# A hybrid decoder block on one core: residual rows and half of each attention output added by transfers, and the last recurrence head's gate kept in another buffer

## The chip, the cores and the metric

The kernel runs on one core of a Trainium2 chip. The metric is the device time of one launch in microseconds (us), on the core. TensorE (PE) multiplies matrices into PSUM, VectorE (DVE) and ScalarE (ACT) compute and empty PSUM, GpSimd (POOL) computes on SBUF alone, SyncE (SP) issues transfers (DMAs) that 16 DMA engines carry out. All engines run their own instructions in order and wait for each other by semaphores.

## What is computed

One layer on x with 1024 rows of 1024 columns in float32. After a normalisation one input projection feeds two groups of heads; their outputs are concatenated, go through one output projection, and are added to x. Then follow a normalisation, a SwiGLU network of 2816 hidden columns, and a last normalisation. Cut to what matters here:

```python
u = rmsnorm(h, norm1_w[l])
proj = jnp.einsum('bsd,de->bse', u, w_in[l])
ya = dilated_attention_group(qa, ka, va)          # 8 heads of 64, three patterns merged
yb = hgrn2_group(qb, fb, ib, gb, lb_table[l], hgrn_norm_w[l])   # 4 heads of 128, gated linear recurrence
mixed = jnp.concatenate([ya, yb], axis=-1).astype(h.dtype)
h = h + jnp.einsum('bse,ed->bsd', mixed, w_out[l])
u2 = rmsnorm(h, norm2_w[l])
gu = jnp.einsum('bsd,df->bsf', u2, w_gate_up[l])
gate, up = gu[..., :FFN_HIDDEN], gu[..., FFN_HIDDEN:]
h = h + jnp.einsum('bsf,fd->bsd', jax.nn.silu(gate) * up, w_down[l])
return rmsnorm(h, final_norm_w)
```

In `hgrn2_group` each head's output is normalised and multiplied by `silu(g)`, the gate.

## The kernel before

Matrices are multiplied to float32 accuracy by splitting each operand into a high and a low part (`hi` copies to the rounded format, `lo` subtracts), and multiplying three of the four pairs. The large projections use one level of Strassen.

The program does not issue its instructions directly. `Prog` collects operations with an engine or a choice of engines, a cost, and the buffers that each reads and writes; `schedule` is a list scheduler that plays all operations through on a model of the engines and fixes the order of each engine's queue. An operation has a class (`P.cls`): the recurrence (`hgrn`) is class 0, attention is class 1, the rest is class 2, and within a class the longest remaining chain goes first. A transfer lands, in that model, behind all transfers issued before it, 2.2 us plus its own length after the end of its issue. `flex` lets the planner choose between engines: additions that read PSUM are DVE's alone, copies out of PSUM by `hi` or `act` are ACT's, the scaling of probabilities (`ts`) may go to DVE or POOL. So a change of costs or dependences can change the order of everything behind it.

The stages overlap. The input projection runs first and spills its results to DRAM tensors (`f_d`, `q_d`, `g_d` and so on). The four recurrence heads run beside it. Each `hgrn(h)` keeps the decays `f` and the keys or states `ks` in the buffer `E14`, and the intra-chunk scores `A` and the values `iv` in `E16`. When the scores have been used by the last products (`po`), it loads the gate `g_d` over `A` (line 945), forms the mean squares, POOL takes the power (`rstd_of`, line 379), ACT scales, PE transposes, DVE multiplies by the gate (line 311), and SP stores to `m_d`, the concatenated outputs.

Attention runs over 8 heads and, within each, four blocks `j` of 256 queries. DVE takes the masked maximum of the scores (line 1017), ACT the exponentials, POOL or DVE scale by the reciprocal sum (line 320), PE transposes the probabilities (line 1054), ACT and DVE split them (lines 353 and 307), and PE multiplies with the values. The values' high and low halves stand side by side as 128 columns, so the product `py` is a 128 x 256 PSUM tile whose lower 64 partitions hold the high part's product and whose upper 64 the low part's. The output is the sum of both halves. There are 32 such tiles. The slots `ya` and `yb` are two 256-column parts of a buffer with the tag `lm`. Head groups follow each other two at a time; the last are heads 6 and 7 with blocks 2 and 3.

The output projection (`out_proj`, class 2) fills gaps of PE in the attention. It runs per block of 128 tokens (`t`): first with the blocks of 128 rows 0, 1, 2 of `m_d` (recurrence heads 0 to 2), later with blocks 3 to 6, and last with block 7 (attention heads 6 and 7). Each pass accumulates in PSUM and adds to the residual `ht`, a half (512 columns) at a time, on DVE. The residual starts as x, loaded by four transfers of 1 MB into `E13`, `E6`, `E15` and `E16`. The FFN with its own normalisation follows.

Of the kernel before, what the change touches and what calls it, by code (L numbers as in the profile page):

```python
# [13 lines left out]
AF = mybir.ActivationFunctionType  # L14
OP = mybir.AluOpType
# [5 lines left out]
D = 1024  # L21
# [50 lines left out]
class Prog:  # L72
# [44 lines left out]
    class Clock:  # L117
# [7 lines left out]
        def to(self, t):  # L125
            while t >= (self.win + 1) * self.W:
                share = self.busy / self.W
                self.fast = share > 0.42 if self.fast else share > 0.84
                self.win, self.busy = self.win + 1, 0.0
# [123 lines left out]
def hymba_block(ctx: ExitStack, tc: tile.TileContext, x, norm1_w, w_in, lb_logits, hgrn_norm_w, w_out,  # L253
                norm2_w, w_gate_up, w_down, final_norm_w, cos, sin, amask, lmask, eye, out):
    nc = tc.nc
    x = x[0]
    out = out[0]
# [5 lines left out]
    P = Prog()  # L263
# [5 lines left out]
    def moved(nbytes, run):  # L269

        return nbytes / run * (0.008 + run / 27e3) / 16

    def dma(o, i, nbytes, run=2048):
        r = [i] if isinstance(i, (View, Buf)) else []
        w = [o] if isinstance(o, (View, Buf)) else []
        gi = i if r else (lambda: i)
        go = o if w else (lambda: o)
        P.op("SP", 0.5, lambda: nc.sync.dma_start(go(), gi()), r, w, nbytes=moved(nbytes, run))

    def mm(items, r, w):  # L280
        cost = sum(4 * n / 2400.0 + 0.008 if f32 else n / 2400.0 + (0.0132 if n > 128 else 0.007)
                   for o, lt, rh, st, sp, n, m, f32 in items)

        def fn():
            for o, lt, rh, st, sp, n, m, f32 in items:
                nc.tensor.matmul(o(), lt(), rh(), start=st, stop=sp, skip_group_check=True)  # L286
        P.op("PE", cost, fn, r, w)
# [9 lines left out]
    def bank_of(x):  # L297
        return (x.buf if isinstance(x, View) else x).pool == "ps"

    def two(n, psum=False):  # L300

        dve = ("DVE", 0.07 + n * 1.04e-3, not psum)
        return [dve] if psum else [dve, ("POOL", 0.17 + n * 2.1e-3, True)]

    def tt(eng, o, a, b, op, n, f=1.0):
        alts = two(n, bank_of(a) or bank_of(b) or bank_of(o) or op == OP.max)
        P.flex(alts, lambda e: ENG[e].tensor_tensor(o(), a(), b(), op=op), [a, b], [o])  # L307
# [16 lines left out]
    def act(o, a, func, n, scale=1.0, bias=None, accum=None):  # L324
        r, w, kw = [a], [o], {}
        cost = (0.06 if a.buf.pool == "ps" else 0.095) + n * 0.83e-3
        for k, s in (("scale", scale), ("bias", bias)):
            if isinstance(s, View):
                r.append(s)
                cost += 0.09  # L330
        if accum is not None:
            w.append(accum)
            cost += 0.09

        def fn():
            kw = {}
            if isinstance(scale, View) or scale != 1.0:
                kw["scale"] = scale() if isinstance(scale, View) else scale
            if bias is not None:
                kw["bias"] = bias()  # L340
            if accum is not None:
                kw["accum_out"] = accum()
            nc.scalar.activation(o(), a(), func, **kw)  # L343
        P.op("ACT", cost, fn, r, w, aset=SETS.get(func))
# [16 lines left out]
    whole = lambda b: b.v(lambda t: t)  # L361
# [9 lines left out]
    lm = P.buf("lm", [128, 10, 64], I32)  # L371
# [24 lines left out]
    def bank(stream, shape=(128, 512)):  # L396
        names = BANKS[stream]
        while True:
            n = rot[stream] = rot.get(stream, -1) + 1
            tag = f"b{names[n % len(names)]}"  # L400
            if tag not in held:
                return P.buf(tag, list(shape), F32, "ps")

    def turn(name, n):
        rot[name] = rot.get(name, -1) + 1
        return rot[name] % n
# [10 lines left out]
    def E(i, shape, dt=F32):  # L417
        return P.buf(f"E{i}", shape, dt)

    def colv(b, a, n, key):  # L420
        return b.v(lambda t: t[:, a:a + n], key)
# [10 lines left out]
    m_d = P.buf("m_d", [D, S], F32, "dr")  # L432
# [73 lines left out]
    def mm3(o, lh, ll, rh, rl, start, stop, n, m=128):  # L506
        return [(o, lh, rh, start, False, n, m, False), (o, lh, rl, False, False, n, m, False),
                (o, ll, rh, False, stop, n, m, False)]
# [321 lines left out]
    def hgrn(h):  # L830
        rs = slice(h * 128, h * 128 + 128)
        f, ks = colv(E14, 0, S, 0), colv(E14, S, S, 1)
        qp = colv(E15, 0, S, 0)
        A, iv = colv(E16, 0, S, 0), colv(E16, S, S, 1)
# [19 lines left out]
        def scores(n, g):  # L854

            ps = bank("h", (128, 2, 192))
            mm([(ps.v(lambda b, c=c: b[:, c, :n]), cs(ks, 2 * g + c),
                 E15.v(lambda t, c=c: t[:, S + (2 * g + c) * 192:S + (2 * g + c) * 192 + n]),
                 True, True, n, 128, True) for c in range(2)], [half(ks, g // 2), E15.v(None, 1)], [ps])
            return ps  # L860
# [31 lines left out]
        for g in range(4):  # L892
            ps = scores(192, g)
# [7 lines left out]
        for i, l in enumerate((1, 3, 5)):  # L901
# [8 lines left out]
            for g in range(4):  # L910
                ps = scores(192, g)
# [14 lines left out]
        for g in range(2):  # L926
            ps = bank("h")
# [9 lines left out]
        for c in range(NT):  # L937
            o = pj(po[c // 4], c % 4)
# [3 lines left out]
                it.append((o, cs(qp, c), cs(ks, c - 1), False, True, 128, 128, True))  # L942
                rd += [half(qp, c // 4), half(ks, (c - 1) // 4)]
            mm(it, rd, [o])
        gt = A
        dma(gt, g_d.v(lambda b: b[rs, :], h), 128 * S * 4)
        ss = P.buf("hss", [128, NT])
        for g in range(2):
# [14 lines left out]
    ys = []  # L963
# [23 lines left out]

    def attention(h, js):
        G = h // 4
        yb, ya = ys  # L990
        EQ, EV = EA[h % 2]
        qs, kh = colv(EQ, 0, S, 0), colv(EQ, S, S, 1)
        vv, kl = colv(EV, 0, S, 0), colv(EV, S, S, 1)
# [5 lines left out]
        for j in js:  # L999
            pr = {}  # L1000
            for b in (2 * j, 2 * j + 1):
                mx = None
                for g in range(b // 4 + 1):
                    n = min(512, (b + 1) * 128 - g * 512)
                    ps = bank("s")
# [6 lines left out]
                    p = probs()  # L1012
                    pn = p.buf.v(lambda t, p=p, n=n: p.get(t)[:, :n], p.key)
                    m = P.buf("mx%d" % turn("mx", 6), [128, 1])
                    o = 896 - b * 128 + g * 512
# [11 lines left out]
                for g in range(ng):  # L1027
                    p, pn, n = pr[b, g]
# [5 lines left out]
                for g in range(ng):  # L1034
                    p, pn, n = pr[b, g]
                    ts("POOL", pn, pn, whole(ri), 0.0, n)
            py = bank("y", (128, 256))
            for m2 in range(j + 1):
                diag = m2 == j
                n = 384 if diag else 512  # L1040
                pt = bank("t")
                many, col, rd = [], 0, set()
                for kb in (2 * m2, 2 * m2 + 1):
                    for b in (2 * j, 2 * j + 1):
                        if kb <= b:
                            p = pr[b, kb // 4][0]
# [22 lines left out]
                    it.append((py.v(lambda t, oc=oc: t[:, oc]), EV.v(lambda t, kb=kb: t[:, kb * 128:kb * 128 + 128], 0),  # L1069
                               tl.v(lambda t, cc=cc: t[:, cc]), False, last, nn, 128, False))  # L1070
                mm(it, [vh, vl, th, tl], [py])
            act(yb, py.v(lambda t: t[64:128, :]), AF.Copy, 256)
            act(ya, py.v(lambda t: t[:64, :]), AF.Copy, 256)
            tt("POOL", ya, ya, yb, OP.add, 256)
            dma(m_d.v(lambda b, j=j: b[512 + h * 64:576 + h * 64, j * 256:j * 256 + 256], (4 + h // 2, j // 2, h % 2, j % 2)), ya, 64 * 256 * 4, 1024)

    P.cls = 0
    for h in range(4):
        hgrn(h)
    P.cls = 1  # L1080
    yab = P.buf("lm", [64, 512])
    ys += [colv(yab, 256 * i, 256, i) for i in range(2)]
    dma(amv, amask, 128 * 1920 * 4)
    for h, js in [(h + i, js) for h in (0, 2, 4) for js in ((0, 1, 2), (3,)) for i in range(2)] + [
            (6, (0, 1)), (7, (0, 1)), (6, (2, 3)), (7, (2, 3))]:
        attention(h, js)
# [24 lines left out]
    def out_proj(t, *parts):  # L1111
        ht = hp[t]
        ks = [k for _, p, _ in parts for k in p]
        for n in range(2):
            ps = bank("o")
            for m, k, off in [(m, k, off) for m, p, off in parts for k in p]:
                lh, ll = (v.buf.v(lambda b, v=v, off=off: v.get(b)[:, off:off + 128]) for v in m[k])
                rh, rl = (v.buf.v(lambda b, v=v, n=n: v.get(b)[:, n * 512:n * 512 + 512], v.key) for v in WO[k])
                mm(mm3(whole(ps), lh, ll, rh, rl, k == ks[0], k == ks[-1], 512), [*m[k], *WO[k], *([before] if n else [])], [ps])
            before = ps  # L1120
            hn = ht.buf.v(lambda b, n=n: ht.get(b)[:, n * 512:n * 512 + 512], ht.key + (n,))
            tt("DVE", hn, whole(ps), hn, OP.add, 512)

    for k0 in (4, 6):
        wo(k0)
    for i in range(4):
        b = E((13, 6, 15, 16)[i], [128, 2, D])
        dma(b, x.rearrange("(t p) n -> p t n", p=128)[:, 2 * i:2 * i + 2, :], 1 << 20)
        for k in range(2):
            hp[2 * i + k] = b.v(lambda t, k=k: t[:, k, :], k)  # L1130
    for t in range(NT):
        if t in (5, 6):
            wo(0 if t == 5 else 2)
        out_proj(t, (mix(0, 3, t * 128, 128), (0, 1, 2), 0))
    for t in range(4):
        out_proj(t, (mix(3, 4, t * 128, 128), (3, 4, 5, 6), 0))
    ml = mix(7, 1, 0, 512)
    for t in range(4):
        out_proj(t, (ml, (7,), t * 128))
# [19 lines left out]
    for t in range(NT):  # L1159
        ht = hp[t]  # L1160
# [12 lines left out]
        if t >= 3 and len(leads) < LEAD:  # L1173
            p, up = gseq[len(leads)]
# [214 lines left out]
```

## Time and profile before

| | us |
|---|---|
| median of 3 runs | 1249.33 (1248.32 to 1254.5) |
| the profiled execution, device time | 1252.68 |
| its span from first to last instruction | 1250.9 |

The profiled execution was 3.35 us above the median. Its mean granted clock of TensorE was 0.994 of full speed. Durations below are from this execution alone. "Busy" for PE counts matmuls that overlap, so an engine shown busy all the time may still be waiting inside its queue; the weight loads (PEld) stand in a column of their own. The issue of a transfer does not count as busy, and the time from issue to landing is listed separately. A line such as L307 is a helper's line and stands for all its callers; the names of the tiles tell them apart (buffer numbers are left out, so `lm` is the slots of the attention output, `m_d` the concatenated outputs in DRAM, `E` any large buffer, `b` a PSUM bank).

### The profile page before, as it was taken

To read this page: it belongs to the slowest core of one execution; us is meant where nothing else is said; L and a number is where in the kernel's file an instruction comes from. 1 tells how busy PE (TensorE), PEld (TensorE's weight loads), DVE (VectorE), ACT (ScalarE), POOL (GpSimd) and SP (SyncE) were. 2 spreads that over 40 slices of the span, in tenths; PEclk is the share of its full clock that TensorE was granted. 3 is DMA by queue.
4 is the path that set the end of the run, shared out by engine and by line. 5 is a ranking of instruction groups with operands and counts; after the bars stand their busy time and mean duration, and the time that the engine had idled before them with its cause. 6 is when DMAs were issued, how large, how long until landed. Compare 5 with 4: busy or idle time off the path is not lost.

```text
span 1250.9 us, 17947 instructions
## 1 busy us (share of the span) xinstructions
PE 1211.4 (97%) x6244; PEld 1032.8 (83%) x6244; DVE 1025.4 (82%) x2113; ACT 475.9 (38%) x1015; POOL 120.7 (10%) x216
## 2 busy tenths in 40 slices
PE   4999999999988999999999999999999999999997
PEld 4888889888988888987888888888888887888885
DVE  6999989998779999966888676676776769978986
ACT  5642332344326888841732132221222222223222
POOL 1110000101004454410100000000000000000001
PEclk9999999999989999999999999999999999999999
DMA  8334443514448753325223322323323369534433
GB/s 265 130 131 161 176 145 96 189 68 155 141 140 282 210 156 88 110 62 185 94 76 126 118 94 92 127 85 110 126 81 105 109 238 370 176 110 127 135 109 118
DMA packets 132522, 175.57 MB, mean 140 GB/s; under 512 B 18512, under 2 KB 85200, under 8 KB 132432
## 3 DMA queue, kind: packets, MB, share of 16 engines
q1 hardware_dynamic: 132432, 174.43, 42.7%
q8 instruction: 49, 0.80, 0.3%
q14 instruction: 41, 0.34, 0.1%
HBM read 122.76 MB, written 51.64 MB: 139 GB/s over the span
## 4 chain that ended last, share of the span: by engine, by line
PE 61%; DVE 4%; ACT 1%; issue 1%; POOL 1%; DMA 0%; DVEq 0%; POOLq 0%; ACTq 0%
PE b L286 59%; PE b L1054 2%; DVE E L307 1%; DVE wh L1017 1%; DVE wl L307 1%; ACT wh L343 0%; DMA m_d<-lm 0%; ACT wl L353 0%; PE b L292 0%; DVE E L311 0%; DVE lm L307 0%; ACT E L343 0%; DVE wh L320 0%; ACT lm L343 0%; ACT E L353 0%
## 5 line engine op out<-in xcount | busy, mean ns | idle before, releaser
L286 PE MATMUL b<-E,wh 128*128 128x512 f32 (+1 forms) x2096 | 643.3, 388 | 4.8 <-ACT wl L343 1.9
L286 PEld LDWEIGHTS b<-E,wh 128*128 128x128 f32 x2096 | 385.6, 188 | 82.7 <-DVE E L307 4.4
L286 PE MATMUL b<-E,wl 128*128 128x512 f32 (+1 forms) x1048 | 403.5, 385 | 0.0
L353 ACT ACTIVATE wh<-st 128x512 fp32r<-128x512 f32 (+1 forms) x203 | 127.1, 630 | 384.4 <-PE b L286 207.0
L307 DVE TENSOR_TENSOR wl<-st,wh 128x512 fp32r<-128x512 f32 x335 | 227.7, 690 | 6.8 <-ACT wh L353 3.5
L286 PEld LDWEIGHTS b<-E,wl 128*128 128x128 f32 x1048 | 197.1, 188 | 39.7
L307 DVE TENSOR_TENSOR E<-b,E 128x512 f32<-128x512 f32 (+1 forms) x157 | 105.9, 684 | 37.7 <-PE b L286 35.5
L355 DVE TENSOR_SCALAR wh<-st 128x512 fp32r<-128x512 f32 x125 | 52.8, 425 | 89.2 <-PE b L286 86.3
L286 PE MATMUL b<-wl,wh 128*128 128x512 f32 x308 | 119.9, 389 | 0.5 <-DVE wl L307 0.5
L286 PE MATMUL b<-wh,wl 128*128 128x512 f32 x308 | 119.9, 389 | 0.1
L286 PE MATMUL b<-wh,wh 128*128 128x512 f32 x308 | 119.8, 389 | 0.0
L286 PE MATMUL b<-wl,E 128*128 128x256 f32 (+1 forms) x544 | 115.9, 287 | 1.1 <-DVE wl L307 1.1
L286 PE MATMUL b<-E,E 128*128 128x192 f32 (+3 forms) x464 | 100.5, 327 | 4.5 <-DVE E L311 3.7
L307 DVE TENSOR_TENSOR wl<-b,wl 128x512 f32<-128x512 f32 (+2 forms) x139 | 89.8, 653 | 16.3 <-PE b L286 13.6
L307 DVE TENSOR_TENSOR st<-st 128x512 f32<-128x512 f32 x136 | 93.1, 689 | 0.7
L286 PEld LDWEIGHTS b<-wl,E 128*128 128x128 f32 x544 | 88.3, 192 | 4.3 <-DVE wl L307 1.5
L343 ACT ACTIVATE E<-E 128x512 f32<-128x512 f32 (+2 forms) x77 | 54.3, 706 | 97.6 <-DVE E L307 43.6
L286 PE MATMUL b<-wh,E 128*128 128x256 f32 x448 | 89.3, 291 | 0.1
L286 PEld LDWEIGHTS b<-E,E 128*128 128x128 f32 x464 | 76.1, 194 | 10.6 <-DVE E L311 3.9
L355 POOL TENSOR_SCALAR wh<-st 128x512 fp32r<-128x512 f32 (+1 forms) x15 | 10.2, 678 | 742.3 <-PE b L286 662.8
L286 PEld LDWEIGHTS b<-wh,E 128*128 128x128 f32 x448 | 72.6, 193 | 0.7 <-DVE wh L307 0.3
L286 PEld LDWEIGHTS b<-wl,wh 128*128 128x128 f32 x308 | 57.8, 188 | 13.0 <-DVE wl L307 1.0
(140 smaller groups left out, 1407.3 us busy)
## 6 DMA issues: line engine op xcount, KB each, us to landing
st<-in_w_gate_up_dram SPq DMA_DIRECT2D x22, 1024.0 KB, 5.2
st<-a_d SPq DMA_DIRECT2D x77, 256.0 KB, 3.0
st<-in_w_in_dram SPq DMA_DIRECT2D x16, 1024.0 KB, 5.6
a_d<-E SPq DMA_DIRECT2D x45, 256.0 KB, 2.2
E<-in_w_down_dram SPq DMA_DIRECT2D x44, 256.0 KB, 5.4
E<-in_x_dram SPq DMA_DIRECT2D x8, 512.0 KB, 9.1
E<-qs_d SPq DMA_DIRECT2D x32, 128.0 KB, 4.1
E<-kh_d SPq DMA_DIRECT2D x32, 128.0 KB, 4.1
```

What stands on the lines that cost most here:

```text
L286: nc.tensor.matmul(o(), lt(), rh(), start=st, stop=sp, skip_group_check=True)
L307: P.flex(alts, lambda e: ENG[e].tensor_tensor(o(), a(), b(), op=op), [a, b], [o])
L343: nc.scalar.activation(o(), a(), func, **kw)
L353: nc.scalar.activation(o(), i(), AF.Copy)
L355: ENG[e].tensor_scalar(o(), i(), 1.0, 0.0, op0=OP.mult, op1=OP.add)
L1017: nc.vector.tensor_tensor_reduce(pn(), pv(), am()[:, o:o + n], 1.0, -3e38 if mx is None else mx(), op0=OP.add, op1=OP.max, accum_out=m()),
L1054: nc.tensor.transpose(ov(), iv(), ident())
```

## The change

Three edits, and what they need:

- Only in the last recurrence head (`h == 3`) the gate is loaded over `f` instead of `A`.
- The attention output tile is copied by one ACT instruction with all 128 partitions into a slot (two slots in turn). SP stores the lower 64 partitions to `m_d`; POOL then issues a transfer that adds the upper 64 partitions to the same place of `m_d`. That transfer reads what the first one wrote, so it waits for its landing.
- The first pass of the output projection (the one with block 0) copies PSUM to `ht`, on ACT or DVE as the planner chooses, and POOL then issues a transfer that adds 128 rows of x from DRAM to `ht`. The four loads of x on SP go away.

```diff
@@ hgrn
-        gt = A
+        gt = f if h == 3 else A
         dma(gt, g_d.v(lambda b: b[rs, :], h), 128 * S * 4)
@@ attention
-        yb, ya = ys
...
-            act(yb, py.v(lambda t: t[64:128, :]), AF.Copy, 256)
-            act(ya, py.v(lambda t: t[:64, :]), AF.Copy, 256)
-            tt("POOL", ya, ya, yb, OP.add, 256)
-            dma(m_d.v(lambda b, j=j: b[512 + h * 64:576 + h * 64, j * 256:j * 256 + 256], (4 + h // 2, j // 2, h % 2, j % 2)), ya, 64 * 256 * 4, 1024)
+            y = ys[turn("y2", 2)]
+            act(y, whole(py), AF.Copy, 256)
+            to = m_d.v(lambda b, j=j: b[512 + h * 64:576 + h * 64, j * 256:j * 256 + 256], (4 + h // 2, j // 2, h % 2, j % 2))
+            dma(to, y.buf.v(lambda t, y=y: y.get(t)[:64, :], y.key), 64 * 256 * 4, 1024)
+            P.op("POOL", 0.9, lambda to=to, y=y: nc.gpsimd.dma_start(out=to(), in_=y.get(y.buf())[64:128, :], accum_op=OP.add),
+                 [y, to], [to], nbytes=moved(64 * 256 * 4, 1024))
...
-    yab = P.buf("lm", [64, 512])
+    yab = P.buf("lm", [128, 512])
@@ out_proj
-            tt("DVE", hn, whole(ps), hn, OP.add, 512)
+            if 0 in ks:
+                P.flex([("ACT", 0.06 + 512 * 0.83e-3, False), ("DVE", 0.07 + 512 * 1.04e-3, False)], lambda e, o=hn, i=whole(ps):
+                       nc.scalar.activation(o(), i(), AF.Copy) if e == "ACT" else nc.vector.tensor_copy(o(), i()), [ps], [hn])
+            else:
+                tt("DVE", hn, whole(ps), hn, OP.add, 512)
+        if 0 in ks:
+            P.op("POOL", 0.9, lambda ht=ht, t=t: nc.gpsimd.dma_start(
+                out=ht(), in_=x[t * 128:t * 128 + 128, :], accum_op=OP.add), [ht], [ht], nbytes=moved(128 * D * 4, 4096))
...
-        dma(b, x.rearrange("(t p) n -> p t n", p=128)[:, 2 * i:2 * i + 2, :], 1 << 20)
```

## Rows read from the trace of the kernel before

**Rows 1.** The page's first part: busy time, share of the span, instructions.
```profile
PE 1211.4 (97%) x6244; PEld 1032.8 (83%) x6244; DVE 1025.4 (82%) x2113; ACT 475.9 (38%) x1015; POOL 120.7 (10%) x216
```

**Rows 2.** Loads of x, 370 to 412 us: issue ns min/median/max, first and last start.
```profile
L278 SPq DMA_DIRECT2D E<-in_x_dram x4: 372/378/489, 374.6 to 408.5; - x4
```

**Rows 3.** Last attention store, and a later split: start, length, instruction [idle before].
```profile
551.30 0.51 SPq L278 DMA_DIRECT2D m_d<-lm  x1
...
556.96 0.63 ACT L353 ACTIVATE wh<-st 128x512 fp32r<-128x512 f32 x1 [6.61 <-DMA st<-m_d]
```

**Rows 4.** Busy time by stage; the first line names the columns.
```profile
core 0: us, PE busy (x) PEld busy (x) DVE busy (x) ACT busy (x) POOL busy (x), PEclk, DMA share, GB/s
400.00:552.00 152.00, 150.26 (x972) 133.57 (x973) 144.50 (x434) 122.97 (x330) 67.65 (x134) 0.99 0.46 131
...
395.00:412.00 17.00, 14.38 (x79) 11.89 (x78) 16.22 (x50) 13.47 (x46) 8.52 (x15) 0.90 0.71 221
...
436.00:485.00 49.00, 47.49 (x315) 42.12 (x314) 47.99 (x159) 40.15 (x112) 23.15 (x47) 1.00 0.45 123
485.00:552.00 67.00, 67.00 (x435) 59.78 (x434) 61.58 (x179) 53.73 (x141) 26.70 (x56) 1.00 0.34 96
552.00:620.00 68.00, 65.38 (x339) 54.20 (x338) 47.20 (x81) 26.43 (x50) 6.08 (x12) 1.00 0.43 141
800.00:850.00 50.00, 50.00 (x222) 41.43 (x221) 34.61 (x59) 12.62 (x22) 0.00 (x0) 1.00 0.34 116
```

**Rows 5.** The same view, two stretches of 5 us where attention takes over.
```profile
395.00:400.00 5.00, 2.61 (x10) 1.19 (x8) 4.59 (x20) 4.63 (x20) 3.68 (x6) 1.00 0.97 329
400.00:405.00 5.00, 4.98 (x27) 4.84 (x28) 4.93 (x14) 4.56 (x15) 2.52 (x4) 0.66 0.60 182
```

**Rows 6.** PE's waits from 388 to 412 us: total, times, longest.
```profile
PE b L286 <- DVE mx L1017: 2.6, 3, 1.3
```

**Rows 7.** The chain that ended last: start, length, what; one piece each way.
```profile
400.04 1.12 DVE E L307
...
546.72 13.72 PE b L286 x66
```

**Rows 8.** Around the last head's gate, from the same view.
```profile
393.81 0.57 SPq L278 DMA_DIRECT2D E<-g_d  x1
...
401.21 1.91 PE L292 MATMUL b<-ident,E 128*128 128x128 f32 x8
...
402.69 0.73 DVE L311 SCALAR_TENSOR_TENSOR E<-b,hw,E 128x512 f32<-128x512 f32 x1
```

**Rows 9.** The gate before it; below, the last gate's landing time, us min/median/max.
```profile
350.07 0.75 DVE L311 SCALAR_TENSOR_TENSOR E<-b,hw,E 128x512 f32<-128x512 f32 x1 [6.76 <-DMA E<-g_d]
...
DMA to landing us min/median/max: 4.4/4.4/4.4
```

**Rows 10.** Groups from 400 to 552 us: busy, mean ns, idle before them.
```profile
L320 POOL TENSOR_SCALAR wh<-wh,ri 128x512 f32<-128x512 f32 (+3 forms) x58 | 40.8, 708 | 31.3 <-DVE ri L1033 18.7 <-PE b L286 4.6 <-ACT lm L343 3.3
...
L343 ACT ACTIVATE lm<-b 64x256 f32<-64x256 f32 x62 | 23.4, 377 | 7.0 <-DMA m_d<-lm 2.9 <-PE b L286 2.8 <-DVE lm L307 0.4
...
L307 DVE TENSOR_TENSOR E<-b,E 128x512 f32<-128x512 f32 x20 | 13.5, 676 | 2.0 <-PE b L286 1.7 <-issue 0.3
L320 DVE TENSOR_SCALAR wh<-wh,ri 128x512 f32<-128x512 f32 (+3 forms) x32 | 13.5, 434 | 0.3
L307 DVE TENSOR_TENSOR lm<-lm 64x256 f32<-64x256 f32 x28 | 12.5, 445 | 0.4 <-ACT lm L343 0.3
```

**Rows 11.** The same stretch with shapes apart: an ACT copy out of PSUM.
```profile
L353 ACT ACTIVATE wl<-b 128x512 fp32r<-128x512 f32 x47 | 27.7, 591 | 4.5 <-PE b L1054 4.0
```

**Rows 12.** Transfers of `m_d`, columns of rows 2; time to landing, us min/median/max.
```profile
L278 SPq DMA_DIRECT2D m_d<-lm x32: 445/451/543, 397.8 to 551.3; - x32
...
DMA to landing us min/median/max: 1.9/2.8/7.0
```

**Rows 13.** Issues from 412 to 430 us: count, KB, median us to landing.
```profile
m_d<-lm SPq DMA_DIRECT2D x3, 64.0 KB, 4.1
```

## The prediction

> **What bounds the kernel now.** I read the page first. PE is busy for 97% of the span, DVE for 82%, ACT for 38%, POOL for 10% [rows 1]. The change takes no matmul away, so it can only give back time in which PE did not work at its pace, and it can only take effect where its operations stand. The first instruction that it touches is the first load of x at 374.6 us [rows 2], the last attention store is issued at 551.3 [rows 3]. So the second view is busy time by stage between these.
>
> From 400 to 552 us PE shows 150.26 of 152 us, DVE 144.50, ACT 122.97, POOL 67.65 [rows 4]. Two engines are near full. Where does PE wait? From 395 to 412 it is idle for 17.00 - 14.38 = 2.62 us, from 436 to 485 for 1.51, from 485 to 552 for nothing [rows 4]; the first two are also all of it, since 2.39 from 395 to 400 [rows 5] and 1.74 from 400 to 552 [rows 4] add up to the same 4.13. The hole at 395 to 400 (2.61 of 5 us busy) is followed by a stretch whose granted clock is 0.66 [rows 5]: between the levels 2.4 and 1.2 GHz that is (1 - 0.66)/0.5 = 68% of 5 us at the lower one, and (1 - 0.66) x 5 = 1.7 us of work lost. Together **4.13 + 1.7 = 5.8 us are what the attention stage can give back**, 0.46% of the time. The reader should see how small this is beside the busy times that the change removes.
>
> Who makes PE wait there? The three waits from 388 to 412 are for DVE's masked maximum [rows 6], and the chain goes through DVE at 400 us, with a weight split; from 485 on it is PE, for example 13.72 us without a break at 546.72 [rows 7]. So DVE matters in the first part, PE in the second.
>
> PE's busy column overstates, and the Trainium skill says so ("Trainium Kernel Development and Optimization", Performance Expectations): the weight loads' share is the better measure. In the stage it is 133.57 of 152 us, 88%, which by that rule leaves 18 us of room. But in the FFN, where PE has no gap, it is 41.43 of 50 us, 83% [rows 4]; a full PE does not show 100% here. I take 5.8 us from the gaps, not 18.
>
> **The change, part by part.**
>
> *Gate of the last head.* Before, its load is issued at 393.81, once the scores are free, and lands in 4.4 us, at 398.2. The multiplication that needs it runs at 402.69, behind PE's transposes, which begin only at 401.21 [rows 8, 9]. So the gate is there 4.5 us early, and loading it earlier gives 0. The stall of 6.76 us behind a gate at 350 us [rows 9] belongs to head 2, which the change leaves as it is. The load still is one issue; it moves ahead a few places in SP's queue and shares DMA engines with other loads. Bounds: no gain, and a loss of at most its issue, 0.57 us; I take 0, since 4.5 us cover it.
>
> *Attention output.* Removed are 32 of 64 ACT copies of 64 x 256 (62 of them after 400 us, 377 ns each) and the additions, 28 on DVE at 445 ns, 12.5 us, in this stage [rows 10]. The copy that stays has the same columns on twice the partitions; its price lies between that of a 64 x 256 copy, 377 ns, and that of a 128 x 512 one, 591 ns [rows 10, 11]; I take 377, as columns are equal. ACT is relieved by 32 x 0.377 = 12 us. ACT has waited 2.9 us in four places for the slot to be stored [rows 10]; a slot is now held through a second landing, about 2.8 + 1.0 + 2.8 = 6.6 us [rows 12], but there are two in turn, and with a tile every 152/32 = 4.75 us one is wanted again after 9.5. Added are 32 issues on POOL, priced below.
>
> *Residual.* Eight blocks of two halves make 16 additions out of PSUM on DVE, 676 ns each [rows 10], 10.8 us. In their place stand 16 copies. On ACT they cost 591 ns each [rows 11], 9.5 us, about what ACT has just been given; on DVE about what the additions cost, so nothing is won. Four loads of 1 MB leave SP's queue, and 8 transfers of 512 KB join POOL's. No wait for x shows in the stage, so its landing is not what bounds; the added transfers have until the second pass of the same tokens, which adds to `ht` on DVE as before.
>
> *Sum on DVE.* Between 12.5 us (copies all on DVE) and 12.5 + 10.8 = 23.3 us of 144.5 fall away. This does not come out as time: it is free to shorten only PE's 5.8 us. From 436 to 485 DVE is the late one (47.99 of 49 us busy), and I count all 1.5 us of idle as won. At 395 to 412 the chain also runs through weight splits and the last head's normalisation, which stay; about two additions, 0.9 us, lie before PE has restarted, and that is what I count. Next late is PE itself. **Gain: 2.4 us**, bounds 0 and 5.8.
>
> *POOL's issues.* No transfer is issued by POOL in this trace, so its price must be bounded. From below: SP's issue of the same transfer, 0.45 us [rows 12]. From above: as long as that store takes to land at worst, 7.0 us [rows 12], were POOL to stay with it. I take 1.0 us, nearer to SP's issue, since the issue of the same transfer is the nearest row, and twice it, since nothing here shows POOL doing it. 40 x 1.0 = 40 us; POOL has 152 - 67.65 = 84 us free [rows 4], so they fit, up to 84/40 = **2.1 us each**. Each output's issue also waits at the head of POOL's queue for the store to land, usually 2.8 us [rows 12]. Behind it on POOL stand the next scalings of probabilities (58 of 90 are POOL's [rows 10]); for these PE's transposes wait. The planner charges 2.2 us and the length for a landing, and so puts other work before the issue; what is left is the error of its estimate. I take 0 for it, bounds 0 and, in the burst where three stores took 4.1 us [rows 13], 1.3 us over the usual.
>
> *The end.* An attention output reaches `m_d` later: one copy (0.38) and one addition (0.45) less, one POOL issue (1.0) and one more landing (2.8) more: +3.0 us. The last store at 551.30 is followed by the load and by ACT's split at 556.96 [rows 3]. PE runs on without it until 546.72 + 13.72 = 560.4 [rows 7], so 3.5 us cover the delay, and block 7 of `m_d` is the last operand used in any pass. If that cover is gone, it costs up to 3 us. I count 0.
>
> Sum: -2.4 us. The profiled execution would go from 1252.68 to 1250.3. It lies 3.35 us above the median, so I put the median at 1249.33 - 2.4 = **1247**.
>
> **The rivals.**
>
> *All of it comes back (faster).* Fewer DVE operations also let the planner pull the weight splits and with them the filler matmuls into the hole at 395 us: all 5.8 us, and of the 68 - 65.38 = 2.6 us idle behind the attention [rows 4] as well: 8.4 us, 1241. For it: DVE is the releaser of PE's waits. Against: the hole has several causes. By the weight-load rule it would even be 18 us, 1231; that has little for it, as the FFN row shows.
>
> *POOL becomes the bound (slower).* The place is the head of POOL's queue in the attention stage. With 1.0 us per issue, 44 us stay free, so it decides when POOL waits for stores more than 44/32 = 1.4 us on average. Before that point single waits already hurt: PE has no slack after 485 us, and if 8 outputs near the loads of new heads wait 1.3 us each [rows 13], 10 us of stalls reach PE, less the 2.4 won: +8, 1257. Were it the whole 2.8 us on all 32, POOL would need 67.65 + 40 + 90 = 198 us, 46 more than the stage has.
>
> A POOL instruction could also be stretched by DVE. Held by one scaling of 434 ns each [rows 10], 40 issues take 57 us and still fit in 84. The Trainium skill ("SBUF — State Buffer", SBUF: two separate sides) says that a GpSimd transfer's descriptors cannot be written while DVE runs in a two-port mode, and gives 620 ns against about 3100 ns; by that figure an estimate is 2.5 us more per issue, which would not fit: 40 x 3.5 + 67.65 = 208 us, 56 over. No run here shows it, and I give it little.
>
> *No relief (no change).* The planner puts the copies on DVE, and because POOL is charged for 40 issues, moves some 20 scalings from POOL to DVE at 434 ns: +8.7 us against -12.5. DVE stays near 141 us, PE's gaps stay: 1249.
>
> **How the numbers follow.** Forecast 1247 (1244 to 1250): 0.37. All comes back, 1241: 0.20; the weight-load rule: 0.02. POOL bound, 1257: 0.19; the two-port rule: 0.02. No relief, 1249: 0.20. About 0.5%, 6.2 us, is what a measurement of this kernel tells from no change: below 1243.1 is faster, above 1255.6 slower. So faster 0.22, same 0.37 + 0.20 = 0.57, slower 0.21. The range goes from the first rival to the POOL case, 1240 to 1258.
>
> **What would show it.** Right: DVE well under 140 us in the stage, no `lm` addition on DVE, first-pass copies on ACT, PE without gaps from 410 to 550, POOL waiting for stores by under 1 us. The gate's multiplication still behind the transposes. Wrong: PE or ACT waiting for POOL's scalings behind a transfer; issues of over 2 us; a new gap after the last attention store, where block 7 is loaded late; more scalings on DVE. A gain of over 6 us would mean that gaps outside 395 to 552 us had closed, which nothing in my sum explains.

## The result, and the profile after

The changed kernel takes 1262.2 us in the median (1261.29 to 1263.76, 6 runs), the kernel before took 1252.11 (1248.32 to 1254.83) beside it. The ratio is 1.0087, 95% interval 1.0070 to 1.0103: about 11 us slower, where 1247 was forecast and 1258 was the end of the range. Below, a ratio is always to the kernel before on the same chip, as recorded, and "us" behind it is (ratio - 1) x 1251. It is not the quotient of the two medians (here 1.0081); the two differ by up to 0.002, about 2.6 us, most for `res_only` (1.0096 by medians) and `no_wait` (1.0087) of the table below. Slow runs are left out of all ratios: one of `no_wait` (4770 us) and one of the kernel before (1517 us).

The profiled execution took 1262.64 us, its span 1260.9. The page's first part, as [rows 1]:

```profile
PE 1212.9 (96%) x6244; PEld 1033.2 (82%) x6244; DVE 1021.9 (81%) x2107; ACT 466.2 (37%) x991; POOL 138.1 (11%) x222
```

Busy time by stage, with the columns of [rows 4], and two of the holes:

```profile
400.00:552.00 152.00, 140.26 (x899) 123.88 (x900) 133.21 (x414) 109.04 (x294) 77.91 (x133) 0.98 0.69 157
395.00:412.00 17.00, 14.75 (x95) 12.62 (x96) 15.93 (x52) 13.77 (x46) 10.83 (x18) 1.00 0.40 98
436.00:485.00 49.00, 45.09 (x292) 39.39 (x290) 45.60 (x141) 34.73 (x96) 27.57 (x46) 1.00 0.82 180
485.00:552.00 67.00, 62.28 (x394) 55.33 (x393) 56.35 (x176) 46.73 (x127) 33.08 (x59) 0.95 0.58 125
552.00:620.00 68.00, 65.39 (x338) 54.29 (x337) 42.07 (x72) 22.17 (x43) 7.31 (x13) 1.00 0.43 133
...
470.00:480.00 10.00, 7.93 (x52) 6.76 (x51) 7.06 (x25) 7.60 (x20) 4.84 (x8) 1.00 0.80 153
...
515.00:520.00 5.00, 2.96 (x11) 2.71 (x12) 2.58 (x10) 1.77 (x5) 1.66 (x3) 0.67 0.49 116
```

PE is busy for 140.26 of the 152 us, 150.26 before [rows 4]: **the whole loss is here**, and the stage behind (65.39 against 65.38) has none. No engine has become the bound: DVE went from 144.50 to 133.21, POOL stands at 77.91 of 152. What rose is a column that the forecast did not use, the DMA engines' share: 0.46 before, 0.69 now. From 515 to 520 us the granted clock is 0.67, in a hole of PE (2.96 of 5 us); before, 0.66 followed the hole at 395 us [rows 5].

Groups of the same stretch, as [rows 10] (busy, mean ns, idle before them):

```profile
L320 POOL TENSOR_SCALAR wh<-wh,ri 128x512 f32<-128x512 f32 (+3 forms) x45 | 33.2, 770 | 17.3 <-DVE ri L1032 10.8 <-PE b L1053 2.0 <-ACT lm L343 1.7
...
L1075 POOL DMA_DIRECT2D m_d<-lm x28 | 23.8, 862 | 35.2 <-ACT wl L353 13.1 <-DMA m_d<-lm 12.4 <-DVE mx L1016 3.2
...
L320 DVE TENSOR_SCALAR wh<-wh,ri 128x512 f32<-128x512 f32 (+3 forms) x42 | 20.6, 500 | 0.2
...
L343 ACT ACTIVATE lm<-b 128x256 f32<-128x256 f32 x29 | 10.9, 376 | 13.7 <-PE b L286 7.0 <-issue 4.5 <-PE b L1053 1.6
...
L1129 POOL DMA_DIRECT2D E<-in_x_dram x8 | 8.5, 1066 | 0.7 <-ACT lm L343 0.7
...
L1125 ACT ACTIVATE E<-b 128x512 f32<-128x512 f32 x11 | 6.5, 592 | 1.3 <-PE b L286 1.3
...
L1125 DVE COPY E<-b 128x512 f32<-128x512 f32 x5 | 3.4, 684 | 0.0
```

The parts are as planned: one copy in place of two, 11 of 16 first-pass copies on ACT, a POOL issue at 0.86 us. But POOL is idle for 35.2/28 = 1.26 us before each issue for an upper half. The row puts 12.4 of the 35.2 us down to the store and 13.1 to an ACT split that this issue does not read; at least one of the latter is the store too, as the second piece of the chain below shows: it lands at 504.88, and POOL issues at 505.42 after standing 5.15 us. How much of the rest is the store is not shown. DVE has taken 10 more scalings (42 for 32), +7.1 us.

The chain that ended last, two pieces (start, length, what):

```profile
452.66 5.92 DMA m_d<-lm
...
459.10 0.09 POOL m_d L1075
...
459.70 0.98 POOL wh L320
...
460.73 1.09 PE b L1053 x8
```

```profile
498.00 6.88 DMA m_d<-lm
...
504.90 0.38 SPq L278
...
510.44 6.46 DMA E<-kl_d
516.90 0.14 issue
517.03 3.01 PE b L286 x10
```

Ahead of the two stores transfers of x were issued, at 450.08 and 494.69, and ahead of the keys another at 507.94. In the first piece the store lands after 5.92 us (median before 2.8 [rows 12]); POOL stays with the issue behind it, then comes a scaling, then PE. In the second the chain goes from the store's landing through SP's issues of the heads' loads, and PE waits for the last heads' low keys, which take 6.46. Such keys are what PE waits for most from 400 to 552 us (total, times, longest; before, none of its waits there was for a load):

```profile
PE b L286 <- DMA E<-kl_d: 5.2, 4, 3.2
```

So the trace names two suspects: POOL's **hold** at the head of its queue, and the **load** on the DMA engines that lengthens every landing. A third is the planner's other order.

### The profile page after: what moved, and what is told of

It reads as the page before. It is cut to its first block, busy times and chain, and to the rows that moved or that the text cites. A ratio compares the mean times of both kernels' runs of the same rounds, so it can differ in the third digit from the quotient of the medians.

```text
span 1260.9 us, 17972 instructions
## 1 busy us (share of the span) xinstructions
PE 1212.9 (96%) x6244; PEld 1033.2 (82%) x6244; DVE 1021.9 (81%) x2107; ACT 466.2 (37%) x991; POOL 138.1 (11%) x222
## 4 chain that ended last, share of the span: by engine, by line
PE 78%; DVE 9%; DMA 7%; ACT 2%; issue 1%; SPq 1%; POOL 0%; DVEq 0%; POOLq 0%; ACTq 0%
PE b L286 76%; DMA m_d<-lm 2%; DVE wl L307 2%; DVE E L307 2%; PE b L1053 2%; DMA E<-kl_d 1%; DMA st<-in_w_in_dram 1%; SPq L278 1%; DVE E L870 1%; DMA E<-in_w_down_dram 1%; PE b L292 1%; DVE wh L307 1%; DVE E L311 1%; DVE st L307 1%; DVE wh L1016 1%
## 5 line engine op out<-in xcount | busy, mean ns | idle before, releaser
L307 DVE TENSOR_TENSOR E<-b,E 128x512 f32<-128x512 f32 (+1 forms) x141 | 95.0, 684 | 38.9 <-PE b L286 37.0
```

## The experiments

Each kernel was run beside the kernel before on the same chip.

| kernel | ratio, 95% interval | us |
|---|---|---|
| the changed kernel | 1.0087 (1.0070 to 1.0103) | +10.9 |
| gate_only | 0.9992 (0.9976 to 1.0009) | -1.0 |
| att_only | 1.0026 (1.0007 to 1.0045) | +3.3 |
| res_only | 1.0076 (1.0055 to 1.0096) | +9.5 |
| no_wait | 1.0066 (1.0043 to 1.0088) | +8.3 |
| res_nox | 1.0023 (1.0008 to 1.0038) | +2.9 |
| res_plain | 1.0050 (1.0027 to 1.0073) | +6.3 |
| after_nox | 1.0013 (0.9994 to 1.0031) | +1.6 |
| after_thin | 0.9992 (0.9976 to 1.0007) | -1.0 |
| after_late | 1.0092 (1.0074 to 1.0109) | +11.5 |
| after_priced | 1.0027 (1.0013 to 1.0041) | +3.4 |
| after_px | 1.0063 (1.0042 to 1.0085) | +7.9 |
| res_priced | 1.0041 (1.0025 to 1.0057) | +5.1 |
| priced_thin | 1.0005 (0.9989 to 1.0022) | +0.6 |
| after_double | 1.0151 (1.0127 to 1.0176) | +18.9 |
| replan | 1.0022 (1.0009 to 1.0035) | +2.8 |
| psum_add | 1.0024 (1.0009 to 1.0039) | +3.0 |

**Which edit.** Each of the three edits alone, cut from the diff above, `gate_only`:

> The kernel before with the gate edit alone. All theories but one: the last head's gate was there 4.5 us early, so nothing changes: within 3 us of the kernel before. If the gate edit were what costs the 10 us (its load now among other loads), this kernel alone would show +5 us or more.

`att_only`:

> The kernel before with the attention output edit alone (loads of x stay four transfers on SP). Held-queue theory (POOL waits at the head of its queue for the lower half's store to land, with scalings of probabilities behind it): +6 to +10 us, POOL idle before its transfers about 1.3 us each. Contention theory (the accumulating transfers of x lengthen the landings of stores and of new heads' loads): +3 us at most, since x is loaded as before. Re-planning theory (the planner charges POOL and orders all else worse): about +5 us here and about as much with the residual edit alone.

`res_only`:

> The kernel before with the residual edit alone: copies and eight accumulating transfers of x on POOL, attention outputs as before. Held-queue theory: -2 to +2 us. Contention theory: +5 to +10 us, with landings of m_d and of the new heads' keys (kl_d) as long as in the changed kernel (4 to 8 us in the bursts, 6 to 7 us for kl_d at 490 to 530 us).

The gate is free. The loss is the residual edit's, +9.5 of +10.9 us, although it has no wait of POOL for a store; the attention edit gives +3.3, although POOL is idle for 27.6/31 = 0.89 us before each of its issues in this stage. That speaks for the load. In the trace of `res_only`, which keeps the old slots, the same lengthened store holds another engine. A transfer of x is issued at 420.38, the store at 424.18; ACT:

```profile
425.02 0.38 ACT L343 ACTIVATE lm<-b 64x256 f32<-64x256 f32 x1 [0.71 <-PE b L286]
430.07 0.38 ACT L343 ACTIVATE lm<-b 64x256 f32<-64x256 f32 x1 [3.02 <-DMA m_d<-lm]
```

ACT's copy stands 3.02 us at the head of its queue until the slot is stored; DVE, whose addition needs that copy, is idle for 2.40 us, and PE then has to wait 2.3 us for DVE's maximum.

**The hold taken away.** `no_wait` writes the upper half to another tensor:

```diff
+            up = m2_d.v(lambda b, j=j: b[h * 64:64 + h * 64, j * 256:j * 256 + 256], (h, j))
-            P.op("POOL", 0.9, lambda to=to, y=y: nc.gpsimd.dma_start(out=to(), in_=..., accum_op=OP.add), [y, to], [to], ...)
+            P.op("POOL", 0.9, lambda to=up, y=y: nc.gpsimd.dma_start(out=to(), in_=...), [y], [up], ...)
```

> The changed kernel, but POOL writes the upper half of each attention output into a tensor of its own by a plain transfer of the same size; it adds nothing and waits for no store. Left out is the addition of the low part's product to the attention output. Same issues on POOL, same bytes written, no wait at the head of POOL's queue. Held-queue theory: all or most of the loss goes, at most +3 us over the kernel before, PE busy from 400 to 550 us back to 48 to 50 of 50 us in each row. Contention theory: it stays at +7 to +10 us. If it is the issue itself that costs, also +7 to +10 us.

It keeps +8.3. POOL's issues no longer wait for a store, and PE's waits of 400 to 552 us still name the heads' loads (total, times, longest):

```profile
PE b L286 <- DVE mx L1017: 4.0, 3, 1.8
PE b L286 <- DMA E<-kl_d: 2.8, 3, 2.1
PE b L286 <- DMA E<-qs_d: 2.2, 1, 2.2
```

So the hold, which was my first theory behind the result, falls as the main cause (the planner's order is another here, so a part of 2 to 3 us can't be excluded by this run); it is one of the places where the load is felt.

**The transfers of x taken away, or made plain.**

```diff
-        if 0 in ks:
-            P.op("POOL", 0.9, lambda ht=ht, t=t: nc.gpsimd.dma_start(
-                out=ht(), in_=x[t * 128:t * 128 + 128, :], accum_op=OP.add), [ht], [ht], ...)
```

> The residual edit alone, without its eight transfers of x: left out is the addition of x to the residual. The copies out of PSUM and everything else stay as with the residual edit alone. Transfer theory (what costs is the x transfers, which lie among the stores and the new heads' loads and lengthen their landings): back to the kernel before, -4 to +2 us. Re-planning or copy theory (ACT is given 16 copies, and the order of the rest changes): stays at +6 to +12 us.

> The changed kernel without its eight transfers of x: left out is the addition of x to the residual. Transfer theory: what is left is the attention output edit, so 0 to +4 us over the kernel before, and POOL's wait for the lower half's store, about 1.3 us each in the changed kernel, goes under 1 us. Held-queue theory by itself: it stays at +7 us or more.

> The residual edit alone, with its eight transfers of x at the same places and of the same size, but plain: x is written over the first pass's result instead of added to it (left out is that first product in the residual). If the bytes and their place in time cost: +7 to +12 us as with the residual edit alone. If it is the adding that costs (the accumulating queue took 15.5% of the 16 DMA engines from 400 to 560 us for 4.19 MB, the others 41.5% for 18.23 MB, so about 1.6 times as much per byte): +3 to +6 us.

Without them +2.9 and +1.6 are left, the first a little above the transfer theory's +2; POOL's idle time before each upper half falls to 24.9/31 = 0.80 us in `after_nox`. Plain ones come out between (+6.3 against +9.5, though the intervals of the two overlap); clearer is what they take of the DMA engines from 400 to 560 us (packets, MB, share of 16 engines). Adding, then plain:

```profile
q0 software_dynamic: 1152, 4.19, 15.5%
```

```profile
q0 software_dynamic: 1152, 4.19, 8.4%
```

15.5% of 160 us is 24.8 us, 3.1 us of all 16 engines for each transfer, against 1.7 for a plain one: 1.85 times as much for the same bytes, in the same order of instructions. The Trainium skill ("Collectives: The Full Stack", The bandwidth ceiling: the fold count and why AG ≠ RS ≠ AR) tells of the adding in a collective on a ring of four ranks that each chunk needs two reads where a copy needs one, and gives a measured 1.93 between the bandwidths of the two. The 1.85 here lies near it; that second reads are the cause, no run here shows.

**The same order without the bytes.** `res_nox` and `after_nox` give the planner fewer operations, so their orders can be others; `after_thin` settles it: every engine's order is that of the changed kernel, but a transfer of x moves 16 columns.

```diff
-                out=ht(), in_=x[t * 128:t * 128 + 128, :], accum_op=OP.add)
+                out=ht()[:, :16], in_=x[t * 128:t * 128 + 128, :16], accum_op=OP.add)
```

> The changed kernel in its exact order of instructions on every engine, but each of the eight transfers of x moves 16 of its 1024 columns (left out is the rest of x in the residual); the planner is charged as before. Same issues, same waits, same order, 8 KB in the place of 512 KB. Load theory (what costs is that the bytes of x occupy the DMA engines while stores and new heads' loads are waited for): as without the transfers, 0 to +3 us over the kernel before. Re-planning theory (the order that the planner makes when it is charged for them): +9 to +11 us, as the changed kernel.

-1.0 against +10.9 us: **in this order the bytes of x are the loss, 11.9 us; the same order, issues and waits without them lose nothing.** The stage, the group of issues and the landings in its trace (the last column of the issues is the median us to landing):

```profile
400.00:552.00 152.00, 151.05 (x983) 134.28 (x982) 137.72 (x426) 112.03 (x298) 81.65 (x137) 1.00 0.56 137
```

```profile
L1075 POOL DMA_DIRECT2D m_d<-lm x31 | 26.4, 859 | 23.7 <-ACT wl L353 11.1 <-ACT wh L353 4.5 <-ACT lm L343 4.0
```

```profile
E<-qs_d SPq DMA_DIRECT2D x24, 128.0 KB, 3.3
E<-kh_d SPq DMA_DIRECT2D x24, 128.0 KB, 3.5
...
m_d<-lm SPq DMA_DIRECT2D x31, 64.0 KB, 2.2
```

PE's wait for the last heads' low keys, 5.2 us in the changed kernel:

```profile
PE b L286 <- DMA E<-kl_d: 0.2, 1, 0.2
```

The landings in the changed kernel:

```profile
E<-in_x_dram POOLq DMA_DIRECT2D x8, 512.0 KB, 7.6
E<-qs_d SPq DMA_DIRECT2D x24, 128.0 KB, 5.0
E<-kh_d SPq DMA_DIRECT2D x24, 128.0 KB, 5.3
...
m_d<-lm SPq DMA_DIRECT2D x29, 64.0 KB, 3.0
```

PE gets 151.05 of 152 us. POOL still stands 23.7/31 = 0.76 us before each upper half, and no loss shows: half a microsecond more of it, and heads' loads 1.7 us later, is what the traces show between the two. `after_thin` also loads 4 MB less than the kernel before, so its -1.0 is not a clean measure of what the edits gain.

**Another place.** `after_late` issues the transfers behind the last heads' loads:

```diff
-        if 0 in ks:
+        if (0 if t > 3 else 3) in ks:
-                out=ht(), in_=..., accum_op=OP.add), [ht], [ht], ...)
+                out=ht(), in_=..., accum_op=OP.add), [ht, m_d.v(None, (6, 0)), m_d.v(None, (6, 1))], [ht], ...)
```

> The changed kernel with its transfers of x moved: for the first four token blocks behind the second pass, for the others until heads 4 and 5 are stored; so all eight stand behind the last heads' loads, in a stretch where the DMA engines were busy for 0.2 to 0.4 of the time. Load theory: the place decides, so most of the 9 us that the transfers cost go: 0 to +5 us over the kernel before. If the bytes cost wherever they stand, or the later passes now wait for x: +8 to +12 us.

+11.5: the expectation of the load theory missed. POOL's timeline shows the costliest place (start, length, instruction [idle before]):

```profile
516.06 0.87 POOL L1129 DMA_DIRECT2D E<-in_x_dram  x1
...
517.23 3.28 POOL L1129 DMA_DIRECT2D E<-in_x_dram  x3
...
532.97 0.62 POOL L355 TENSOR_SCALAR wh<-st 128x512 fp32r<-128x512 f32 x1 [8.12 <-DMA st<-m_d]
```

```profile
515.00:533.00 18.00, 15.95 (x102) 13.74 (x100) 13.69 (x46) 9.29 (x25) 8.39 (x14) 1.00 0.85 165
533.00:552.00 19.00, 14.64 (x88) 13.38 (x89) 12.59 (x31) 12.14 (x31) 9.39 (x18) 0.82 0.40 80
...
530.00:535.00 5.00, 0.95 (x5) 0.48 (x3) 0.00 (x0) 0.66 (x2) 2.03 (x5) 1.00 0.29 61
```

```profile
PE b L1053 <- DVE wl L307: 6.4, 1, 6.4
```

Four were issued from 516.06 to 520.51. The load of `m_d` for the next pass, issued among them at 518.55, took 14.26 us; POOL, in order, stood 8.12 us before its split, with the scalings behind it, and PE waited 6.4 us at one stroke, all of its idle time from 515 to 552 us. Behind it the granted clock was 0.82 from 533 to 552 us, (1 - 0.82) x 19 = 3.4 us of work more. These 9.8 us are most of the 11.5. The stretch was quiet only as long as nothing was put there.

**The planner's prices.** It reckons 1.28 us for a transfer of x (the trace: 3.1) and 0.18 for an upper half. For the latter `att_only` shows 12.3% of 160 us for 32, 0.62 each. `after_priced` has both prices, `after_px` and `res_priced` that of x alone, `priced_thin` the order of `after_priced` with 16 columns, `after_double` twice both.

```diff
-            ... accum_op=OP.add), [y, to], [to], nbytes=moved(64 * 256 * 4, 1024))
+            ... accum_op=OP.add), [y, to], [to], nbytes=0.62)
-                ... accum_op=OP.add), [ht], [ht], nbytes=moved(128 * D * 4, 4096))
+                ... accum_op=OP.add), [ht], [ht], nbytes=3.1)
```

> The changed kernel with the planner charged what the traces show of the adding transfers (3.1 us of all 16 DMA engines for each of x, where it reckoned 1.28; 0.62 for each upper half, where it reckoned 0.18). Same work. If the loss comes from the planner's ignorance of what these transfers take: +2 to +7 us over the kernel before. If it is the load itself, which no order within the classes escapes: +8 to +12 us.

> The changed kernel with the planner charged 3.1 us for each transfer of x (where it reckoned 1.28), the upper halves as it had them. If it is the price of x that the planner lacked: +2 to +5 us over the kernel before, as with both prices. If it was the price of the upper halves: +8 to +11 us.

> The residual edit alone with the same price of 3.1 us for each transfer of x. If the wrong price is the cause of the residual edit's loss: +2 to +5 us, as without the transfers (+2.9). If with both prices it was an order that came out well by luck: +7 to +11 us, as with the residual edit alone.

> The order of the kernel with both prices, exactly, but its transfers of x move 16 of 1024 columns (left out is the rest of x in the residual). The difference to that kernel is what the bytes of x still cost when the planner knows of them: if the price settles it, 0 to 3 us less than its +3.4; if the load still costs as in the changed kernel (11 us between full and thin transfers in the same order): -6 us or below.

> Both prices doubled (6.2 us for x, 1.24 for an upper half). If the planner needs the landing under load (6 to 8 us for x) rather than the occupancy: 0 to +2 us over the kernel before. If 3.1 is the right price, an overcharge delays other work: +4 to +8 us.

With both prices the same bytes cost 3.4 - 0.6 = 2.8 us, not 11.9, although they take the same share of the DMA engines, 0.69 as in the changed kernel (`after_priced`):

```profile
400.00:552.00 152.00, 148.39 (x958) 130.52 (x957) 135.19 (x421) 112.00 (x299) 73.31 (x127) 1.00 0.69 162
```

The issues of x stand 11 to 19 us apart there, in the changed kernel 11 to 22. With the price of x alone 3 of 11 us come back (4.4 of 9.5 in the residual edit; the intervals of each pair touch), and doubled prices cost +18.9, with all eight issues of x within 53 us (425.7 to 478.6), so more charge does not mean more spread. For `after_double` both expectations missed; +7.9 lies next to the band that gave the price to the upper halves, and +5.1 just above the one for x, so these two do not tell which price matters. That the order decides how much of the load is felt is shown; **that the right price makes the good order is not**: it may be one of many that happened to fit.

**What an order is worth.** `replan` changes no work:

```diff
-                end = dma_free + 0.97
+                end = dma_free + 1.4
```

> The kernel before, no work changed, but with the planner's estimate of a transfer's landing 0.43 us longer, so that another order comes out. It shows how far an order that nothing asked for moves the time: the attention output edit, the residual edit without its transfers and the addition straight from PSUM all came out 3 us slower. If those 3 us are of that kind: +2 to +5 us here. If orders are worth nothing: within 1.5 us.

+2.8, and partly in a stage that the change does not touch, from 80 to 120 us (before, then `replan`, in its profiled execution of 1257.51 us, the slowest of its 12):

```profile
80.00:120.00 40.00, 40.00 (x177) 32.62 (x176) 38.82 (x67) 14.18 (x22) 0.62 (x1) 1.00 0.45 151
```

```profile
80.00:120.00 40.00, 37.35 (x158) 30.50 (x157) 36.10 (x61) 10.94 (x18) 1.24 (x2) 0.96 0.37 132
```

In the attention PE is busy for 148.06 of 152 us, 2.2 less than before. It is one order, but enough to say that the +3 of `att_only` and `res_nox` needs no cause of its own: some 3 us between two planner orders say nothing about an edit here. `psum_add` spares the same ACT copy without any transfer:

```diff
-            act(ya, py.v(lambda t: t[:64, :]), AF.Copy, 256)
-            tt("POOL", ya, ya, yb, OP.add, 256)
+            tt("DVE", ya, py.v(lambda t: t[:64, :]), yb, OP.add, 256)
```

> The kernel before with another way to spare half of the attention output copies: ACT copies the upper half out of PSUM, and DVE adds the lower half straight from PSUM (an addition from PSUM in the place of a copy and an addition in SBUF). No transfer is added, no issue on POOL. If relief of ACT and a shorter chain to the store are worth something: -2 to -5 us. If DVE's additions, which now can't go to POOL and read PSUM, are what decides: 0 to +3 us.

+3.0, of the same size: no gain from relieving ACT shows. No version is faster than the kernel before by more than its interval.

## Why the prediction was wrong

- **What bounds the kernel: not contradicted, but one column short.** PE had 5.8 us to give back, and `after_thin`, the change without x's bytes, gains 1.0 (-0.9 to 3.0); the 2.4 counted lies inside, and so does no gain at all, so the 2.4 is not shown. The stage view that carried the argument also has the DMA share; I used it for nothing.
- **Gate, 0: right** (`gate_only`, -1.0 with 0 inside the interval). In the changed kernel its load was issued at 388.01, its multiplication ran at 403.13, still behind PE's transposes at 402.31.
- **Prices: right.** A copy 376 ns (377 taken), an issue 0.86 us for an upper half and 1.07 for x (1.0 taken), 592 ns for a first-pass copy.
- **DVE's relief: too large.** Taken 12.5 to 23.3 us, in the trace 144.50 - 133.21 = 11.3, as 10 scalings moved to DVE (+7.1) and 5 copies stayed there (3.4). The rival without relief had the direction of this step, at twice the size (some 20 scalings, DVE near 141 us), and not the result.
- **The end, +3.0 covered by 3.5: right.** The last store is issued at 557.7, and 552 to 620 us is as before.
- **The residual's transfers, 0: this step failed.** "No wait for x shows in the stage, so its landing is not what bounds; the added transfers have until the second pass of the same tokens, which adds to `ht` on DVE as before." Nobody waits for x in the stage after the change either (the one wait for x in the trace, 2.5 us of ACT, is for the loads at the start of the kernel). But the term was put at 0 because I asked who waits for x, and not whom x delays. The bytes moved from 374 to 412 us, where a burst of other loads stood anyway, into the attention, where they delay stores and heads' loads, and adding makes them take 1.85 times as much of the DMA engines. With the bytes the change costs 10.9 us, in the same order without them -1.0: the term measures 11.9 us, the whole loss. It is 2.8 us in the order of `after_priced`, so its size hangs on the order.
- **The wait at the head of POOL's queue, 0 (bounds 0 to 1.3): the size was off, up to 1.26 us each, but the cause lay in the step above.** With x's bytes gone POOL still stands 0.76 us, and no loss shows.
- **The rival "POOL becomes the bound", 1257**, came nearest in size. Its mechanism, single long waits for stores at the head of POOL's queue, is a part of what happened, but POOL did not bound: without the hold +8.3 was left. Its price was the landing in bursts of the kernel before (4.1 us [rows 13]), whereas the change itself lengthened the bursts (5.9 and 6.9 us in the two pieces of the chain). The price by the rule on the two-port mode does not show: no such issue in the changed kernel took over 1.2 us, beside a DVE busy for 133.21 of 152 us. How many of DVE's instructions ran in that mode, no row shows.

## What to carry to other kernels

When a transfer is moved, ask two questions: who waits for it, and which other transfers share the DMA engines with it at the new place, and who waits for those; the DMA share of that stage is a budget too, though it does not settle the loss by itself: at 0.69 one order lost 10.9 us and another 3.4. An addition that a transfer does is not free: measure what it takes of the DMA engines (here 1.85 times the plain transfer for x, some three times for the upper halves) before counting on it. And before a difference of a few microseconds between two planned orders gets a cause, measure an order that nothing asked for.

## What the runs showed of the hardware

- The same 512 KB from DRAM to SBUF by POOL's queue took 3.1 us of all 16 DMA engines when adding and 1.7 when plain; median landing 6.2 and 4.6 us. POOL's issue took about 0.9 against 0.6 us.
- For the upper halves (64 KB from SBUF to DRAM) adding took 0.62 us of all 16 engines each, in 2560/32 = 80 packets. In `no_wait` they are plain: less the share of x in `res_only`, (19.8% - 15.5%) of 160 us are left for 32, an estimate of 0.21 us each, in (2176 - 1152)/32 = 32 packets. So adding took about three times as much there. First `att_only`, then `no_wait`, 400 to 560 us:

```profile
q0 software_dynamic: 2560, 2.10, 12.3%
```

```profile
q0 software_dynamic: 2176, 6.29, 19.8%
```

- SP's own issues were held up. By the profile SP stood until earlier loads of the heads had landed, from 400 to 560 us in the changed kernel, and then with thin transfers (total, times, longest; before it was 1.6 us):

```profile
SPq L278 <- DMA E<-qs_d: 9.9, 11, 2.5
```

```profile
SPq L278 <- DMA E<-qs_d: 0.8, 2, 0.6
```

So under load the next loads were also issued later. What makes SP wait there was not tried.

- A load of 256 KB issued among four adding transfers of 512 KB took 14.26 us (`after_late`); in `after_thin` the median of such loads is 3.0.
